# Moving the weight and token tiles of a TensorE-bound encoder step to other byte offsets in SBUF

## The chip, the core and the metric

The kernel runs on one core of one Trainium2 chip. The metric is device time in microseconds of one execution. A core has a matrix engine (PE, with its weight loads shown apart as PEld), three elementwise engines (DVE, ACT, POOL), a DMA-issuing engine (SP) and an on-chip memory (SBUF) of 128 partitions. A tile in SBUF has the same byte address in every partition; this document is about that address modulo 256, which it calls the tile's phase.

## The reference, cut to what matters

One layer of a hybrid encoder is applied to 288 tokens, 256 of a new stream and 32 of a running one. In float32 it computes

```
proj = rmsnorm(x) @ w_in                      2048 -> 5664 columns
pool = trailing means of u, times w_pool      4 groups of 256
ssd  = convolution, chunked scan, gate        32 heads
x    = x + rmsnorm([pool, ssd] @ w_out)       3072 -> 2048
up   = rmsnorm(x) @ w_up                      2048 -> 11264
x    = x + rmsnorm((silu(gate) * val) @ w_down)   5632 -> 2048
```

and the new states. Nearly all arithmetic is in four products of 288 tokens with large weights; every weight is used once.

## The kernel before, in words

**The products.** Tokens lie along the moving side of the matmul, 288 at a time; a 128x128 block of weights is the stationary side. Weights and tokens are each split into a high part, rounded to the matmul's format, and a low part, the remainder. One block costs three matmuls (`mm3`, lines 163 to 165): high weights with high tokens, high weights with low tokens, low weights with high tokens. Each of the three issues its own weight load, so the high weights are loaded twice.

```
pe.matmul(out, wh, a[:, 0, :], start=start, stop=False)   # line 163
pe.matmul(out, wh, a[:, 1, :], start=False, stop=False)   # line 164
pe.matmul(out, wl, a[:, 0, :], start=False, stop=stop)    # line 165
```

`project` runs over groups of 256 output columns, then over the inner dimension in stretches of up to eight blocks. For each stretch `fetch_w` (line 131, SP's DMA queue) brings the raw weights, and `split_w` makes tiles `whi` (ACT, line 146) and `wlo` (DVE, line 147) of 1024 elements a partition, four blocks each. Tags `raw`, `hi` and `lo` have four buffers each in the pool `wpool`. A `whi` buffer is written again when the matmuls that read it are done. One narrow group of 32 columns (the time steps) goes through `split_narrow`, whose stationary operand holds high and low weights side by side, 64 columns (lines 187, 188).

**The token tiles** are `[128, 2, 288]`: the high part at the tile's start, the low part 1152 bytes on, which is 128 modulo 256. They are called `xn`, `mixs` and `hn` (pool `apool`), `fa` (pool `ffn`), `mixp` and `du` (pool `outp`).

**Where tiles lie.** Pools are laid out one behind the other: `const`, `wpool`, a 128-byte pool `shift`, `apool`, `bpool`, and then a region used in turn by `xin` (start), `mixer`, `outp` and `ffn`. Tile sizes are rounded to 32 bytes. In the program as laid out, `const` ends so that `wpool` begins at 34784; every `raw`, `whi` and `wlo` buffer begins at 224 modulo 256. All token tiles begin at 96, so their high part lies at 96 and their low part at 224. `outp` ends at 229344 bytes and `ffn` at 228832, close to the end of what a partition has.

**Order.** Within an engine instructions run in a fixed order, drawn up by the planner when the program is built. Work at the start that concerns the change: `scan_one` (POOL memsets, lines 230 and 232), `sel`, `pick` and `sel64` (DVE, lines 236 to 239) are made in `const` before the first DMA issues of POOL's queue. They are read in the mixer: `scan_one` by the scan at line 439, `pick` at lines 472 and 473, `sel64` by a matmul at line 475. `state_out` (line 690) copies transposed states to tiles `so`, which SP's queue stores; line 970 does so with `fso`. The squares for the norms go through tiles `sq` (line 608), which POOL adds up (line 609). `fr` is a product tile of the last stage (lines 923, 924 and 1036).

Of the kernel before, what the change touches and what calls it, by code (L numbers as in the profile page):

```python
# [8 lines left out]
F32 = mybir.dt.float32  # L9
F32R = mybir.dt.float32r  # L10
AF = mybir.ActivationFunctionType
ALU = mybir.AluOpType
AX = mybir.AxisListType
# [3 lines left out]
P = 128  # L17
# [4 lines left out]
NT = NP_ + NS  # L22
# [3 lines left out]
HEADS = 32  # L26
# [3 lines left out]
NX = D_SSD // P  # L30
NF = D_FF // P
# [12 lines left out]
def body(  # L44
# [38 lines left out]
    act, dve, pool, pe, sp = nc.scalar, nc.vector, nc.gpsimd, nc.tensor, nc.sync  # L83
# [10 lines left out]
    const = ctx.enter_context(tc.tile_pool(name="const", bufs=1))  # L94
    wpool = ctx.enter_context(tc.tile_pool(name="wpool", bufs=4))
# [8 lines left out]
    def aux(shape, name):  # L104
        return aux_ps.tile(shape, F32, tag="aux", name=name)
# [4 lines left out]
    def btile(name):  # L110
        return bpool.tile([P, NT], F32, tag="b", name=name)

    def split_from(a, src, scale=None):
# [4 lines left out]
        else:  # L118
# [4 lines left out]
                ),  # L123
            )

    ahead = [0]

    def fetch_w(view, kb, nk, c0, nc_):
# [5 lines left out]
    def split_w(raw, kb, nk, nc_, after=()):  # L134

        out = []
        step = min(nk, 1024 // nc_)
        for k in range(0, nk, step):
            n = min(step, nk - k)
            hi = wpool.tile([P, n, nc_], F32R, tag="hi", name="whi")  # L140
            lo = wpool.tile([P, n, nc_], F32R, tag="lo", name="wlo")
            with ExitStack() as order:
                order.enter_context(tc.high_priority(offset=ahead[0]))
                for ins in after:
                    order.enter_context(tc.issue_after(ins.ins))
                act.activation(hi, raw[:, k : k + n, :], AF.Copy)  # L146
                dve.tensor_tensor(lo, raw[:, k : k + n, :], hi.bitcast(F32), op=ALU.subtract)  # L147
            out.append([(kb + k + i, hi[:, i, :], lo[:, i, :]) for i in range(n)])
        return out
# [17 lines left out]
    def project(view, groups, acts, ksplit, before=None, done=None, spare=0, hold=()):  # L167
# [9 lines left out]
        for i, (kb, n) in enumerate(ksplit):  # L177
            raws = [fetch_w(view, kb, n, c0, w) for c0, w in groups]
            nxt = None
            if before and i + 1 < len(ksplit):  # L180
                nxt = before(*ksplit[i + 1])
            m0 = 0
            for raw, (c0, w) in zip(raws, groups):
                if w < P:
                    for k, both in split_narrow(raw, kb, n, w, after or ()):
                        o = accs[m0][: 2 * w, :]
                        pe.matmul(o, both, acts[k][:, 0, :], start=k == k_first, stop=False)
                        pe.matmul(o, both, acts[k][:, 1, :], start=False, stop=k == k_last)
                    continue
                parts = split_w(raw, kb, n, w, ((after or ()) if m0 else ()) + (hold if i else ()))  # L190
                for q, part in enumerate(parts):
                    for m in range(w // P):
                        c = slice(m * P, (m + 1) * P)
                        for k, hi, lo in part:
                            mm3(accs[m0 + m], hi[:, c], lo[:, c], acts[k], k == k_first, k == k_last)
                        if done and i + 1 == len(ksplit) and q + 1 == len(parts):
                            done(m0 + m, accs[m0 + m])
                m0 += w // P
            after = nxt
# [13 lines left out]
    ident = const.tile([P, P], F32, name="ident")  # L213
# [12 lines left out]
    rec = const.tile([P, 16], F32, name="rec")  # L226
    for t in range(16):
        pool.memset(rec[:, t : t + 1], 1.0 / (t + 1))
    scan_one = const.tile([HEADS, NT], F32, name="scan_one")
    pool.memset(scan_one, 1.0)  # L230
    for c in range(0, NT, 64):
        pool.memset(scan_one[:, c : c + 1], 0.0)
    sel = const.tile([HEADS, 2], F32, name="sel")
    pick = const.tile([HEADS, NX], F32, name="pick")
    id32 = ident[:HEADS, :HEADS]
    dve.tensor_reduce(sel, id32.rearrange("h (t r) -> h r t", r=2), axis=AX.X, op=ALU.add)
    dve.tensor_reduce(pick, id32.rearrange("h (t r) -> h t r", r=2), axis=AX.X, op=ALU.add)
    sel64 = const.tile([HEADS, 2, 64], F32, name="sel64")
    dve.tensor_copy(sel64, sel.unsqueeze(2).broadcast_to([HEADS, 2, 64]))

    NE = 4
    ebuf = []
    for i in range(NE):
# [120 lines left out]

    mixer = ExitStack()
    mp = mixer.enter_context(tc.tile_pool(name="mixer", bufs=1))
    sc_stage = const.tile([P, 2, 3, NXC], F32, name="sc_stage")
    np_stage = const.tile([P, 2, 15, NU], F32, name="np_stage")
    hist_c = pb[:, 0:60].rearrange("p (r t) -> p r t", t=NXC)
# [43 lines left out]
    def htile(name, n=NT, tag=None):  # L413
        return mp.tile([HEADS, n], F32, tag=tag or name, name=name, bufs={"z": 4}.get(tag, 2) if tag else 1)
# [23 lines left out]
    r = htile("r", tag="z")  # L438
# [42 lines left out]
    for i in range(4):  # L481
        o = btile("bc")
# [201 lines left out]
    def state_out(stage, n, outs, pool_):  # L684

        for s in range(2):
            p_ = aux([n, P], "pso")
            pe.transpose(p_, stage[:, s, :], ident)
            o = pool_.tile([P, P], F32, tag="so", bufs=2, name="so")
            act.activation(o[:n, :], p_, AF.Copy)  # L690
            sp.dma_start(out=outs[s], in_=o[:n, :])

# [46 lines left out]
    def pool_group(i):  # L739
        raw = fetch_w(wpv, 2 * i, 2, 0, 256)  # L740
        wq = split_w(raw, 0, 2, 256)[0]
        for j in range(2):
            o = acc_ps.tile([P, NT], F32, tag="acc", name="acc")
            c = slice(j * P, (j + 1) * P)
            for k, hi, lo in wq:
                mm3(o, hi[:, c], lo[:, c], uin[2 * i + k], k == 0, k == 1)
            a = op_.tile([P, 2, NT], F32R, name=f"mixp{2 * i + j}")
            split_from(a, o, p_scale[:, 2 * i + j : 2 * i + j + 1])
            mix[2 * i + j] = a
# [46 lines left out]
    for gi in range(2):  # L796
        c = slice(gi * P, (gi + 1) * P)
# [46 lines left out]
    for grp in ((0, 1), (2,), (3,), (4,), (5,), (6,), (7,)):  # L844
        project(
            wov, [(256 * c, 256) for c in grp], mix, [(8, 8), (16, 8), (0, 8)],
            mix_before(grp[0]), lambda m, p_: mix_out(p_),
        )
        if grp[0] < 6:
            for t in range(LATE * (grp[0] - 2) // 4, LATE * (grp[0] - 1) // 4) if grp[0] else ():  # L850
                state_mm(t, *state_in(t))
        elif grp[0] == 6:
            late_in = [state_in(t) for t in range(LATE, NX)]
        if grp[0] == 0:
            sp.dma_start(out=xT, in_=xT_d)
            state_out(sc_stage.rearrange("p s r t -> p s (r t)"), 60, (rows4(new_sconv_p), rows4(new_sconv_s)), op_)
            state_out(np_stage.rearrange("p s r t -> p s (r t)"), 120, (rows4(new_pool_p), rows4(new_pool_s)), op_)
# [10 lines left out]
    for s in range(KD + 1):  # L868
# [3 lines left out]
        if s:  # L872
            t = s - 1
            a = atile("hn")
            hi = act.activation(a[:, 0, :], x1[t], AF.Copy, scale=g_ffn_pre[:, t : t + 1])
            lo = dve.scalar_tensor_tensor(  # L876
                a[:, 1, :], x1[t], g_ffn_pre[:, t : t + 1], a[:, 0, :].bitcast(F32),
                op0=ALU.mult, op1=ALU.subtract,
            )
# [16 lines left out]
    fp = ffn.enter_context(tc.tile_pool(name="ffn", bufs=1))  # L896
# [60 lines left out]
    part = []  # L957
    up_half(0, HALF)
    for m in range(0, KD, 2):
        for p_ in project(wdv[:, 0:HALF, :], [(m * P, 256)], f[:HALF], [(0, 8), (8, 8), (16, 6)]):  # L960
            o = btile("part")
# [3 lines left out]
    for s, o_ in enumerate((new_fconv_p, new_fconv_s)):  # L965
        p_ = aux([2 * NF, 2, P], "pfo")
        for r_ in range(2):
            pe.transpose(p_[:, r_, :], fc_stage[:, s, r_, :], ident)
        so = fp.tile([2 * NF, 2, P], F32, tag="fso", bufs=1, name="fso")
        act.activation(so, p_, AF.Copy)  # L970
        sp.dma_start(out=o_.rearrange("o b r (t p) -> t (o b r) p", p=P), in_=so)

# [6 lines left out]
    for q in range(4):  # L979
        for b in range(2):  # L980
            t = apool.tile([P, 512], F32, tag="a", name="xr")
# [126 lines left out]
```

## Time and profile before

| what | value |
|---|---|
| median of 3 runs | 1377.21 us (1376.95 to 1377.78) |
| the profiled execution, its own time | 1377.7 us |
| its span in the profile | 1376.0 us |
| granted PE clock, mean | 0.994 |
| PE busy | 1355.0 us, 98% |
| DVE busy | 879.3 us, 64% |
| ACT busy | 670.8 us, 49% |
| POOL busy | 240.8 us, 18% |

A matmul's duration in the profile overlaps with the next matmul's, so what tells PE's speed is the distance from one matmul's start to the next one's, or the count of matmuls in a window in which PE never idles. Below, this distance is called the step.

### The profile page before, as it was taken

What the parts mean: (1) busy time and instruction counts of PE and PEld (TensorE: products, weight loads), DVE (VectorE), ACT (ScalarE), POOL (GpSimd) and SP (SyncE); (2) the same over time, 40 slices, a digit from 0 to 9 for tenths busy, and PEclk for the clock granted to TensorE, in tenths of its full rate; (3) what the DMA queues carried; (4) which work ended last, traced back from release to release, by engine and by line L of the source; (5) the groups of instructions that cost most, each with busy time, mean ns of one, the idle gap of its engine ahead of it and who ended that gap; (6) DMA issues with size and microseconds to landing.
All of it is one profiled execution on the core that took longest, in us unless ns stands there. A gap on an engine that the chain in (4) does not pass through costs nothing.

```text
span 1376.0 us, 25874 instructions
## 1 busy us (share of the span) xinstructions
PE 1355.0 (98%) x10247; PEld 1333.0 (97%) x10247; DVE 879.3 (64%) x1551; ACT 670.8 (49%) x1013; POOL 240.8 (18%) x394
## 2 busy tenths in 40 slices
PE   8999999999999999999999999999999999999996
PEld 7999999999999998999999999999999999999995
DVE  6898887669544448877667653334766766654443
ACT  6547767546444345644444443334444444454441
POOL 3122211122123310212112100000211211201110
PEclk9999999999999999999999999999999999999998
DMA  8878875455755634766555455555555545476662
GB/s 270 258 194 262 250 207 171 152 187 176 228 179 175 191 106 146 223 176 194 175 157 178 149 169 169 169 170 161 176 161 171 167 156 181 155 230 184 191 186 86
DMA packets 293287, 250.55 MB, mean 182 GB/s; under 512 B 67344, under 2 KB 286458, under 8 KB 293038
## 3 DMA queue, kind: packets, MB, share of 16 engines
q1 hardware_dynamic: 289962, 242.41, 57.8%
q0 software_dynamic: 2320, 3.86, 0.9%
q10 hardware_dynamic: 884, 2.63, 0.5%
q8 instruction: 80, 1.31, 0.4%
q14 instruction: 41, 0.34, 0.1%
HBM read 234.55 MB, written 14.31 MB: 181 GB/s over the span
## 4 chain that ended last, share of the span: by engine, by line
PE 97%; DVE 2%; issue 0%; DMA 0%; ACT 0%; DVEq 0%
PE acc L163 31%; PE acc L165 31%; PE acc L164 30%; PE pst L824 1%; PE py L555 1%; DVE wlo L147 0%; DVE xr L1066 0%; DVE hn L876 0%; PE py L559 0%; PE py L561 0%; PE py L557 0%; DVE xsum L888 0%; DMA xt<-in_x_prompt 0%; PE pt L299 0%; PE pt L301 0%
## 5 line engine op out<-in xcount | busy, mean ns | idle before, releaser
L147 DVE TENSOR_TENSOR wlo<-raw,whi 128x1024 fp32r<-128x1024 f32 (+1 forms) x414 | 493.9, 1194 | 351.2 <-ACT whi L146 349.8
L146 ACT ACTIVATE whi<-raw 128x1024 fp32r<-128x1024 f32 (+1 forms) x414 | 427.1, 1033 | 518.6 <-PE acc L164 424.8
L163 PE MATMUL acc<-hn,whi 128*128 128x288 f32 x1392 | 409.0, 297 | 2.3 <-ACT whi L146 2.3
L165 PE MATMUL acc<-hn,wlo 128*128 128x288 f32 x1392 | 410.0, 296 | 0.9 <-DVE wlo L147 0.9
L164 PE MATMUL acc<-hn,whi 128*128 128x288 f32 x1392 | 405.4, 292 | 0.0
L163 PEld LDWEIGHTS acc<-hn,whi 128*128 128x128 f32 x1392 | 260.9, 188 | 3.5 <-ACT whi L146 3.4
L165 PEld LDWEIGHTS acc<-hn,wlo 128*128 128x128 f32 x1392 | 260.9, 188 | 1.9 <-DVE wlo L147 1.8
L164 PEld LDWEIGHTS acc<-hn,whi 128*128 128x128 f32 x1392 | 262.2, 188 | 0.2 <-DVE hn L876 0.2
L163 PE MATMUL acc<-xn,whi 128*128 128x288 f32 x704 | 210.1, 300 | 0.0
L163 PE MATMUL acc<-fa,whi 128*128 128x288 f32 x704 | 208.5, 296 | 0.0
L165 PE MATMUL acc<-fa,wlo 128*128 128x288 f32 x704 | 207.4, 295 | 0.0
L165 PE MATMUL acc<-xn,wlo 128*128 128x288 f32 x704 | 207.0, 296 | 0.0
L164 PE MATMUL acc<-xn,whi 128*128 128x288 f32 x704 | 206.8, 295 | 0.0
L164 PE MATMUL acc<-fa,whi 128*128 128x288 f32 x704 | 205.3, 292 | 0.0
L163 PEld LDWEIGHTS acc<-xn,whi 128*128 128x128 f32 x704 | 132.6, 189 | 0.7
L164 PEld LDWEIGHTS acc<-xn,whi 128*128 128x128 f32 x704 | 132.8, 189 | 0.3
L164 PEld LDWEIGHTS acc<-fa,whi 128*128 128x128 f32 x704 | 132.3, 188 | 0.0
L163 PEld LDWEIGHTS acc<-fa,whi 128*128 128x128 f32 x704 | 132.3, 188 | 0.0
L165 PEld LDWEIGHTS acc<-xn,wlo 128*128 128x128 f32 x704 | 131.9, 188 | 0.3
L165 PEld LDWEIGHTS acc<-fa,wlo 128*128 128x128 f32 x704 | 131.7, 187 | 0.0
L909 POOL COPY fc_stage<-ebuf 128x4 f32<-128x4 f32 x88 | 27.5, 312 | 506.0 <-DVE ebuf L908 506.0
L905 POOL COPY ebuf<-pf 128x2 f32<-128x2 f32 x88 | 74.5, 847 | 117.9 <-DVE fc L915 54.0
(308 smaller groups left out, 1635.0 us busy)
## 6 DMA issues: line engine op xcount, KB each, us to landing
raw<-in_w_up SPq DMA_DIRECT2D x82, 1024.0 KB, 5.1
raw<-in_w_in SPq DMA_DIRECT2D x40, 1024.0 KB, 5.6
raw<-in_w_down SPq DMA_DIRECT2D x32, 1024.0 KB, 5.4
raw<-in_w_out SPq DMA_DIRECT2D x24, 1024.0 KB, 5.4
raw<-in_w_down SPq DMA_DIRECT2D x16, 768.0 KB, 4.6
gb<-g_d SPq DMA_DIRECT2D x8, 832.0 KB, 4.9
raw<-in_w_up SPq DMA_DIRECT2D x12, 512.0 KB, 3.6
raw<-in_w_in SPq DMA_DIRECT2D x6, 512.0 KB, 6.4
```

Of the source, the lines that this page charges most:

```text
L146: act.activation(hi, raw[:, k : k + n, :], AF.Copy)
L147: dve.tensor_tensor(lo, raw[:, k : k + n, :], hi.bitcast(F32), op=ALU.subtract)
L163: pe.matmul(out, wh, a[:, 0, :], start=start, stop=False)
L164: pe.matmul(out, wh, a[:, 1, :], start=False, stop=False)
L165: pe.matmul(out, wl, a[:, 0, :], start=False, stop=stop)
L555: pe.matmul(y[c, 0:256], xw[:, 0, c], m[:, j, 0:256], start=True, stop=False)
L824: ins = pe.matmul(st[:, o, :], x_, w, start=i != 1, stop=i != 0)
L905: pool.tensor_copy(e[:, 258:260], pf[:, 4:6, i])
L909: pool.tensor_copy(fc_stage[:, :, :, i], e[:, 256:324].rearrange("p (s c) -> p s c", c=34)[:, :, 0:2])
```

## The change

The change moves data in SBUF and leaves the arithmetic as it is.

- High and low weight tiles come from a helper `wtile`. Each buffer is 1088 elements instead of 1024 (256 bytes more), and the data begin 2 elements (8 bytes) into it for high parts, 34 elements (136 bytes) for low parts.
- `scan_one`, `sel`, `pick` and `sel64` leave `const` for the pool `mixer`, and are made after the start-up pool is closed. `const` is shorter by 1152 + 32 + 64 + 512 = 1760 bytes, so `wpool` begins at 33024, which is 0 modulo 256. High weights then lie at 8, low weights at 136. `wpool` is longer by 8 buffers of 256 bytes, so everything behind it moves by 2048 - 1760 = 288 bytes: token tiles begin at 128, their low part at 0.
- To make room, `so` uses the buffers of tag `sq`, and `fso` those of tag `fr`.

```diff
+    def wtile(part, n, nc_):
+
+        t = wpool.tile([P, 1024 + 64], F32R, tag=part, name="w" + part)
+        d = 2 if part == "hi" else 34
+        return t[:, d : d + n * nc_].rearrange("p (k c) -> p k c", k=n)
+
...
-            hi = wpool.tile([P, n, nc_], F32R, tag="hi", name="whi")
-            lo = wpool.tile([P, n, nc_], F32R, tag="lo", name="wlo")
+            hi = wtile("hi", n, nc_)
+            lo = wtile("lo", n, nc_)
...
-    scan_one = const.tile([HEADS, NT], F32, name="scan_one")
...
-    sel = const.tile([HEADS, 2], F32, name="sel")
-    pick = const.tile([HEADS, NX], F32, name="pick")
...
-    sel64 = const.tile([HEADS, 2, 64], F32, name="sel64")
-    dve.tensor_copy(sel64, sel.unsqueeze(2).broadcast_to([HEADS, 2, 64]))
...
     mp = mixer.enter_context(tc.tile_pool(name="mixer", bufs=1))
+    scan_one = mp.tile([HEADS, NT], F32, name="scan_one")
+    pool.memset(scan_one, 1.0)
+    for c in range(0, NT, 64):
+        pool.memset(scan_one[:, c : c + 1], 0.0)
+    sel = mp.tile([HEADS, 2], F32, name="sel")
+    pick = mp.tile([HEADS, NX], F32, name="pick")
...
+    sel64 = mp.tile([HEADS, 2, 64], F32, name="sel64")
+    dve.tensor_copy(sel64, sel.unsqueeze(2).broadcast_to([HEADS, 2, 64]))
...
-            o = pool_.tile([P, P], F32, tag="so", bufs=2, name="so")
+            o = pool_.tile([P, NT], F32, tag="sq", bufs=2, name="so")[:, :P]
...
-        so = fp.tile([2 * NF, 2, P], F32, tag="fso", bufs=1, name="fso")
+        so = fp.tile([P, NT], F32, tag="fr", bufs=2, name="fso")[: 2 * NF, : 2 * P].rearrange("p (r c) -> p r c", r=2)
```

More of the change, by code (lines that the diff above doesn't have):

```diff
@@ L228, in body @@
         pool.memset(rec[:, t : t + 1], 1.0 / (t + 1))
-    scan_one = const.tile([HEADS, NT], F32, name="scan_one")
-    pool.memset(scan_one, 1.0)
-    for c in range(0, NT, 64):
-        pool.memset(scan_one[:, c : c + 1], 0.0)
-    sel = const.tile([HEADS, 2], F32, name="sel")
-    pick = const.tile([HEADS, NX], F32, name="pick")
-    id32 = ident[:HEADS, :HEADS]
-    dve.tensor_reduce(sel, id32.rearrange("h (t r) -> h r t", r=2), axis=AX.X, op=ALU.add)
-    dve.tensor_reduce(pick, id32.rearrange("h (t r) -> h t r", r=2), axis=AX.X, op=ALU.add)
-    sel64 = const.tile([HEADS, 2, 64], F32, name="sel64")
-    dve.tensor_copy(sel64, sel.unsqueeze(2).broadcast_to([HEADS, 2, 64]))
     NE = 4
@@ L366, in body @@
     mp = mixer.enter_context(tc.tile_pool(name="mixer", bufs=1))
+    scan_one = mp.tile([HEADS, NT], F32, name="scan_one")
[4 more added lines that the diff above has]
+    pick = mp.tile([HEADS, NX], F32, name="pick")
+    id32 = ident[:HEADS, :HEADS]
+    dve.tensor_reduce(sel, id32.rearrange("h (t r) -> h r t", r=2), axis=AX.X, op=ALU.add)
+    dve.tensor_reduce(pick, id32.rearrange("h (t r) -> h t r", r=2), axis=AX.X, op=ALU.add)
+    sel64 = mp.tile([HEADS, 2, 64], F32, name="sel64")
+    dve.tensor_copy(sel64, sel.unsqueeze(2).broadcast_to([HEADS, 2, 64]))
     sc_stage = const.tile([P, 2, 3, NXC], F32, name="sc_stage")
```

## The prediction

> **What bounds the kernel now.** First the engines' totals and the list of who waited for whom:
>
> ```profile
> PE 1355.0 (98%) x10247; PEld 1333.0 (97%) x10247; DVE 879.3 (64%) x1551; ACT 670.8 (49%) x1013; POOL 240.8 (18%) x394
> ```
>
> ```profile
> PE pt L281 <- POOL ebuf L245: 3.6, 1, 3.6
> PE acc L163 <- ACT whi L146: 2.3, 5, 0.7
> PE pt L299 <- DVE xT L304: 1.4, 1, 1.4
> PE acc L165 <- DVE wlo L147: 0.9, 3, 0.5
> PE psum_f L1019 <- ACT fsq L1036: 0.2, 1, 0.2
> ```
>
> PE has work for 98% of the span, and all its waits for others come to 8.4 us. The groups of PE instructions say what the work is; the three lines of `mm3` for one kind of token tile:
>
> ```profile
> L165 PE MATMUL acc<-hn,wlo 128*128 128x288 f32 x1392 | 410.0, 296 | 0.9 <-DVE wlo L147 0.9
> L163 PE MATMUL acc<-hn,whi 128*128 128x288 f32 x1392 | 409.0, 297 | 2.3 <-ACT whi L146 2.3
> L164 PE MATMUL acc<-hn,whi 128*128 128x288 f32 x1392 | 405.4, 292 | 0.0
> ```
>
> With the 704 of `xn`, 704 of `fa`, 256 of `mixs`, 128 of `mixp`, 16 of `du` and 16 that accumulate in `acc_x`, each line has 3,216 matmuls: 9,648 in all. Durations overlap, so the step comes from windows in which PE never idles:
>
> ```profile
> core 0: us, PE busy (x) PEld busy (x) DVE busy (x) ACT busy (x) POOL busy (x), PEclk, DMA share, GB/s
> 0.00:20.00 20.00, 14.93 (x87) 12.94 (x87) 12.41 (x26) 8.78 (x17) 11.96 (x52) 1.00 0.90 279
> 20.00:42.00 22.00, 22.00 (x159) 20.38 (x158) 13.93 (x30) 16.24 (x26) 1.48 (x4) 1.00 0.83 255
> 42.00:112.00 70.00, 70.00 (x526) 68.92 (x526) 64.03 (x146) 39.94 (x67) 15.92 (x24) 1.00 0.80 239
> ...
> 780.00:900.00 120.00, 120.00 (x910) 120.00 (x909) 54.91 (x67) 46.62 (x59) 5.49 (x9) 1.00 0.55 168
> 900.00:1130.00 230.00, 230.00 (x1741) 230.00 (x1741) 139.90 (x229) 103.67 (x136) 32.89 (x56) 1.00 0.52 167
> ```
>
> 230 us / 1741 = 132.1 ns; 120 / 910 = 131.9 ns. DVE is 46% busy in the one and 61% in the other, and the step stays: it isn't set by what other engines do to memory. 9,648 x 132.1 ns = 1274 us of the 1376.0 us span. So the change is worth what it does to this step, and 1 ns of step is 9.6 us, 0.7% of the time. About 0.2%, or 2.8 us, is what a measurement of this kernel can tell from no change; that is 0.3 ns of step.
>
> Now the timeline of PE alone, start and duration in us, in the steady part:
>
> ```profile
> 820.76 0.30 PE L163 MATMUL acc<-fa,whi 128*128 128x288 f32 x1
> 820.90 0.29 PE L164 MATMUL acc<-fa,whi 128*128 128x288 f32 x1
> 821.02 0.29 PE L165 MATMUL acc<-fa,wlo 128*128 128x288 f32 x1
> 821.15 0.29 PE L163 MATMUL acc<-fa,whi 128*128 128x288 f32 x1
> 821.29 0.29 PE L164 MATMUL acc<-fa,whi 128*128 128x288 f32 x1
> 821.42 0.30 PE L165 MATMUL acc<-fa,wlo 128*128 128x288 f32 x1
> 821.55 0.30 PE L163 MATMUL acc<-fa,whi 128*128 128x288 f32 x1
> ...
> 1359.43 0.30 PE L164 MATMUL acc<-fa,whi 128*128 128x288 f32 x1
> 1359.56 0.29 PE L165 MATMUL acc<-fa,wlo 128*128 128x288 f32 x1
> ```
>
> The steps are 0.14, 0.12, 0.13, then 0.14, 0.13, 0.13. The same form of matmul takes 0.12 in one place and 0.14 in another, with nothing to wait for, so part of the 132 ns is stall inside PE. Over the whole trace, leaving out steps over 145 ns, the means are 135.1 ns from L163 to L164 (3,116 steps), 129.4 ns from L164 to L165 (3,156 steps; the last pair of rows above is the last of them), 131.9 ns from L165 to L163 (3,094 steps). The single steps cluster near 126, 132 and 138 ns.
>
> **The change part by part.** *The phases.* While one matmul streams its tokens, the weights of the next are loaded. In the kernel before, the three steps pair tokens and weights at (96, 224), (224, 224), (96, 224): half of 256 apart, together, half apart. Afterwards they are (128, 8), (0, 136), (128, 8): the weights lie 136 beyond the tokens in all three. No row has weights off a multiple of 32, or this distance. What the rows can bound: from 126 ns, the shortest cluster of steps, to 137 ns, the lower edge of the longest. Against the present 132.2 (the mean of the three kinds) that is -6.2 to +5 ns. One more row shows how little the length of the weight load matters: the narrow group loads 64 columns instead of 128,
>
> ```profile
> 37.42 0.30 PE L187 MATMUL acc<-xn,both 128*64 128x288 f32 x1
> 37.55 0.29 PE L188 MATMUL acc<-xn,both 128*64 128x288 f32 x1
> 37.69 0.29 PE L187 MATMUL acc<-xn,both 128*64 128x288 f32 x1
> 37.81 0.29 PE L188 MATMUL acc<-xn,both 128*64 128x288 f32 x1
> 37.95 0.29 PE L187 MATMUL acc<-xn,both 128*64 128x288 f32 x1
> ```
>
> and four steps take 0.53 us, 132 ns each. So a stall that grows with the bytes of the weight load isn't seen; one that depends on where the streams begin relative to each other, or on where the token stream begins in memory, is left. I take 129.4 ns, the mean of the fastest of the three kinds of step, for all of them: a uniform distance should make the three alike, and the trace shows a whole kind of step running at that speed. Gain 132.2 - 129.4 = 2.8 ns.
>
> [...]
>
> How many matmuls gain: until 42 us PE has 87 + 159 records in windows with the DMA engines 83 to 90% busy, so I give that stretch nothing. 9,648 - 246 = 9,400 matmuls x 2.8 ns = 26 us. Others must keep up: from 42 to 112 us DVE works 64.03 us of 70, and a step shorter by 2.1% makes the window 68.5, by 4.7% 66.7; both are still above 64.
>
> *Writers of the shifted tiles.* ACT and DVE now write at 8 and 136, and DVE reads the former. The convolutions read at offsets of 4 and 8 bytes:
>
> ```profile
> L915 DVE SCALAR_TENSOR_TENSOR fc<-ebuf,pf,fc 128x290 f32<-128x290 f32 x176 | 90.5, 516 | 3.5 <-ACT fc L913 0.7
> L121 DVE SCALAR_TENSOR_TENSOR xn<-pt,g,xn 128x288 fp32r<-128x288 f32 x16 | 8.2, 513 | 7.4 <-ACT xn L120 7.4
> ```
>
> 516 ns for 290 elements against 513 for 288 aligned ones: nothing. Were a write 10% dearer, some 24 `wlo` of 1.2 us in that tight window would add 3 us to DVE's 64, still under 68. Zero. The weights' DMAs land at 0 instead of 224 and have slack after 42 us; zero.
>
> *The constants made later.* POOL and DVE at the start:
>
> ```profile
> 1.61 0.17 DVE L236 TENSOR_REDUCE sel<-ident 32x2 f32<-32x32 f32 x1 [1.61 <-POOL ident masks.py:199]
> 1.72 0.17 DVE L237 TENSOR_REDUCE pick<-ident 32x16 f32<-32x32 f32 x1
> 1.82 2.12 DVE L239 COPY sel<-sel 32x128 f32<-32x128 f32 x1
> 2.30 0.33 POOL L230 MEMSET scan_one<- 32x288 f32 x1
> 0.81 3.08 DMA xt<-in_x_prompt
> ```
>
> Taking 0.33 us off POOL's queue ahead of its parameter DMAs, and 2.5 us off DVE, gains nothing on the path: the chain of waits begins with the DMA of `xt`, landed at 3.89 us. Made behind start-up, about 42 us, the same DVE work goes into the window with 6 us of DVE slack; POOL has 54 us there. Behind it on DVE stand the `wlo` splits that PE needs. `pick` is first read at 53.6 us and `scan_one` at 95.1. Cost zero; with the cover gone, 2.5 us.
>
> *`so` in the buffers of `sq`, `fso` in those of `fr`.*
>
> ```profile
> 379.40 0.39 ACT L608 ACTIVATE sq<-acc 128x288 f32<-128x288 f32 x1
> 379.69 0.50 ACT L791 ACTIVATE mg<-acc,pb 128x288 f32<-128x288 f32 x1
> 380.07 0.45 ACT L690 ACTIVATE so<-pso 120x128 f32<-120x128 f32 x2
> 381.83 1.06 ACT L146 ACTIVATE whi<-raw 128x1024 fp32r<-128x1024 f32 x1 [1.31 <-PE acc L164]
> ```
>
> New waits: the copy to `so` waits for POOL's addition of the square before it (1.5 us each), and the next square waits for `so` to be stored (at most 5.3 us to landing). Behind it on ACT stands the next `whi`, and PE behind that. Cover: ACT runs ahead until PE frees a buffer, three tiles of 24 matmuls, 3 x 24 x 132 ns = 9.5 us, against 5.3 + 3 us at worst. Zero; with the cover gone, about 5 us. `fso` waits 2.0 us once today and has two buffers then; zero.
>
> **Sum.** 1377.7 us of the profiled execution - 26 = 1351.4; the runs' median lies 0.5 us lower: 1351.
>
> **The rivals.**
>
> *No change.* The steps are set by something that phases don't touch. For it: in the trace (96, 224) occurs twice, at 135.1 and at 131.9 ns, so the same phases don't have one price, and the first two steps together make 264.5 = 2 x 132.2, as if a constant rate were only unevenly divided. 1377, with 2.8 us to either side. [...]
>
> *Slower: the step in which tokens and weights lie together is the fast one.* Taken literally, the trace has 129.4 ns for (224, 224) and 133.5 as the mean of the two steps half of 256 apart. The change puts the middle step about half apart too. Price 133.5 - 132.1 = 1.4 ns on all, 9,400 x 1.4 = 13 us: 1390. It decides once the new distance is over 0.3 ns dearer than today's mean. Weights off the 32-byte grid could be dearer still: all steps in the longest cluster's neighbourhood, +5 ns, give 1424. Against it: the unequal (96, 224) steps.
>
> *Faster by more.* All steps at 126 ns: 9,400 x 6.2 = 58 us, 1319. For it, only that single steps reach this.
>
> **How the numbers follow.** Faster 0.52: 0.40 near my 1351 (1330 to 1374), 0.12 near 1319. No change 0.10, since a step that varies between clusters will hardly land within 0.3 ns when every phase moves. Slower 0.38: 0.26 near 1390, 0.12 beyond 1396. The range leaves out the last and about half of the far faster case: 1318 to 1396. The likeliest case's own range is 1330 to 1374.
>
> **What would show it.** Right: the window 780 to 900 us, or its counterpart, holds about 927 matmuls instead of 910; the three kinds of step come closer together; counts and durations of `whi` and `wlo` stay. Wrong: 910 as before (phases don't matter), or 900 and fewer (the new distance costs), or new rows of PE waiting for `whi` or `wlo` (ACT held up behind `so`, DVE behind the constants). What would make it wrong is above all the untested 8 bytes.

## The result, and the profile after

The changed kernel takes 1369.0 us (median; 1368.7 to 1369.3) against 1377.1 us before: a ratio of 0.9941, 95% interval 0.9924 to 0.9958. That is 8 us faster, 0.6%, where 26 us were forecast: the right way, a third of the size.

The windows of the changed kernel (columns as in the prediction; the three are those quoted there):

```profile
42.00:112.00 70.00, 70.00 (x533) 69.23 (x532) 66.05 (x150) 37.98 (x56) 18.04 (x30) 1.00 0.76 234
...
780.00:900.00 120.00, 120.00 (x917) 120.00 (x916) 53.49 (x64) 47.65 (x60) 4.67 (x8) 1.00 0.52 162
900.00:1130.00 230.00, 230.00 (x1757) 230.00 (x1756) 143.37 (x237) 104.90 (x140) 34.54 (x60) 1.00 0.52 171
```

917 matmuls where there were 910, and 1757 for 1741: the step is 0.8 to 0.9% shorter in these two stages. 927 would have been the forecast. Earlier the gain is smaller: 0.6% from 270 to 510 us (132.11 to 131.30 ns) and 0.2% from 112 to 270 us (131.69 to 131.42). Over all steps under 145 ns between matmuls of `mm3` the records give 131.23 ns (9,492 steps) against 132.14 (9,488). 9,500 x 0.91 ns = 8.6 us; the two spans differ by 8.8 us (1376.0 and 1367.2). So the step explains the gain, and next to nothing is left for other causes. PE's list of waits is what it was:

```profile
PE pt L275 <- POOL ebuf L239: 3.6, 1, 3.6
PE acc L169 <- ACT whi L152: 2.2, 4, 0.7
PE pt L293 <- DVE xT L298: 1.4, 1, 1.4
PE acc L171 <- DVE wlo L153: 0.9, 3, 0.5
PE psum_f L1024 <- ACT fsq L1041: 0.2, 1, 0.2
```

And the timeline of PE alone after the change (start and duration in us; lines 169 to 171 are the former 163 to 165):

```profile
820.30 0.29 PE L169 MATMUL acc<-fa,whi 128*128 128x288 f32 x1
820.42 0.29 PE L170 MATMUL acc<-fa,whi 128*128 128x288 f32 x1
820.56 0.30 PE L171 MATMUL acc<-fa,wlo 128*128 128x288 f32 x1
820.69 0.29 PE L169 MATMUL acc<-fa,whi 128*128 128x288 f32 x1
820.82 0.29 PE L170 MATMUL acc<-fa,whi 128*128 128x288 f32 x1
820.95 0.30 PE L171 MATMUL acc<-fa,wlo 128*128 128x288 f32 x1
```

Three steps take 0.39 us (820.30 to 820.69, and 820.56 to 820.95), where they took 0.39 and 0.40 in turn. To the nanosecond the three kinds now take 127.1, 131.8 and 134.8 ns in the mean, and over nine in ten of each kind lie within 1.2 ns of that. They have not become alike, though all three have the same distance: (128, 8), written as (tokens, weights) in bytes modulo 256, appears as 127.1 and as 134.8.

### The profile page after: what moved, and what is told of

The parts are those of the page before. It is cut to its first block, busy times and chain, and to the rows that moved or that the text cites. A ratio compares the mean times of both kernels' runs of the same rounds, so it can differ in the third digit from the quotient of the medians.

```text
span 1367.2 us, 25869 instructions
## 1 busy us (share of the span) xinstructions
PE 1346.3 (98%) x10247; PEld 1323.7 (97%) x10247; DVE 878.0 (64%) x1551; ACT 671.0 (49%) x1013; POOL 249.5 (18%) x394
## 4 chain that ended last, share of the span: by engine, by line
PE 97%; DVE 2%; issue 0%; DMA 0%; ACT 0%; DVEq 0%
PE acc L171 31%; PE acc L170 31%; PE acc L169 30%; PE pst L829 1%; PE py L560 1%; DVE wlo L153 0%; DVE xr L1071 0%; DVE hn L881 0%; PE py L564 0%; PE py L566 0%; PE py L562 0%; DVE xsum L893 0%; DMA xt<-in_x_prompt 0%; PE pt L293 0%; PE pt L295 0%
## 5 line engine op out<-in xcount | busy, mean ns | idle before, releaser
L153 DVE TENSOR_TENSOR wlo<-raw,whi 128x1024 fp32r<-128x1024 f32 (+1 forms) x414 | 494.0, 1194 | 346.2 <-ACT whi L152 344.9
L152 ACT ACTIVATE whi<-raw 128x1024 fp32r<-128x1024 f32 (+1 forms) x414 | 427.7, 1034 | 516.7 <-PE acc L170 422.5
L169 PEld LDWEIGHTS acc<-xn,whi 128*128 128x128 f32 x704 | 133.3, 190 | 0.5
L171 PEld LDWEIGHTS acc<-xn,wlo 128*128 128x128 f32 x704 | 132.6, 189 | 0.5
L170 PEld LDWEIGHTS acc<-xn,whi 128*128 128x128 f32 x704 | 132.5, 188 | 0.4
L171 PEld LDWEIGHTS acc<-fa,wlo 128*128 128x128 f32 x704 | 132.2, 188 | 0.0
L170 PEld LDWEIGHTS acc<-fa,whi 128*128 128x128 f32 x704 | 131.7, 187 | 0.0
```

## The experiments

The theory under test: the step is set by where the token stream and the loading weights lie in SBUF. The two do run at the same time: in the trace before, the load of L164's weights begins at 820.76 us, as L163's matmul does, and takes 0.19 us of its 0.30. Rivals: the gain comes from the other edits; from the tokens' own place; from the 8 bytes by themselves. In what follows a pair (tokens, weights) gives phases modulo 256 for the three steps in turn, and "d" is the offset in elements that `wtile` uses. "Half a turn" is 128 bytes, half of 256. Below each run stands, where a reading rests on it, its count of matmuls in the 200 us from 900 to 1100 us; before, there are 1514 (132.1 ns a step), after the change 1528 (130.9).

### Is it the phases at all (e1, e2)?

e1 keeps the later constants and the shared buffers, and fills `const` up so that all phases are the old ones:

```diff
-        t = wpool.tile([P, 1024 + 64], F32R, tag=part, name="w" + part)
-        d = 2 if part == "hi" else 34
+        t = wpool.tile([P, 1024], F32R, tag=part, name="w" + part)
+        d = 0
...
+    hole = const.tile([P, 440], F32, name="hole")
+    pool.memset(hole[:, 0:1], 0.0)
```

> The changed kernel with weights and tokens back at their old phases: tokens 96 and 224, all weights 224; only the later constants and the shared buffers of so and fso are left of the change. If the gain of 8 us comes from phases, this takes the 1377 us of before and its step is 132.1 to 132.2 ns. If it comes from the shorter start, it takes 1369 us with the step of before.

Measured: 1378.5 us against 1378.0 us before, ratio 1.0001 (0.9990 to 1.0011), step 132.12 ns.

```profile
900.00:1100.00 200.00, 200.00 (x1515) 200.00 (x1514) 120.10 (x196) 90.48 (x119) 28.14 (x48) 1.00 0.52 168
```

The other edits are worth nothing.

e2 is the changed kernel with `d = 0` for both parts, so that everything lies 32 bytes on from before and the distances are the old ones.

> The changed kernel with all weights at 0 and tokens at 128 and 0: against before, everything lies 32 bytes further on and the distances of weights and tokens are those of before (128, 0, 128). If the distance decides (the theory of the prediction), 1377 us and a step of 132.2 ns. If the tokens' own phase (on the 128-byte grid) decides, 1369 us and 131.2 ns.

Measured: ratio 0.9996 (0.9984 to 1.0008), step 132.15 ns, and the same three kinds of step as before: 135.1, 129.4, 132.0 (before 135.1, 129.4, 131.9).

```profile
900.00:1100.00 200.00, 200.00 (x1515) 200.00 (x1514) 120.74 (x196) 89.22 (x117) 28.14 (x48) 1.00 0.52 168
```

Moving both streams together by 32 bytes changed nothing here (132.15 ns against 132.14); putting the tokens on a multiple of 128 bytes is not the gain.

### What of the distance counts (e3, e4, e8)?

```diff
-        d = 2 if part == "hi" else 34
+        d = 0 if part == "hi" else 32     # e3: (128, 0), (0, 128), (128, 0)
+        d = 46 if part == "hi" else 14    # e4: (128, 184), (0, 56), (128, 184)
+        d = 2                             # e8: (128, 8), (0, 8), (128, 8)
```

> The changed kernel without the 8 bytes: high weights at 0, low at 128, tokens at 128 and 0, distance 128 in all three steps. If it takes a uniform distance of half of 256 and the 8 bytes add nothing, 1369 us; if the 8 bytes are what matters, 1377 us; if being half apart is the slow case, as the slower rival had it, 1385 us or more.

Measured: 1391.3 us, ratio 1.0086 (1.0065 to 1.0108), step 133.29 ns. The windows of e3:

```profile
780.00:900.00 120.00, 120.00 (x902) 120.00 (x901) 57.87 (x76) 48.48 (x63) 7.59 (x12) 1.00 0.52 163
900.00:1100.00 200.00, 200.00 (x1502) 200.00 (x1501) 115.31 (x182) 87.55 (x115) 25.41 (x44) 1.00 0.51 166
```

902 matmuls in 120 us. With a distance of 128 in all three steps the kernel is slower than before, and 8 bytes more make it faster than before: 22 us lie between e3 and the change.

> The changed kernel with weights 56 beyond the tokens in all three steps (high at 184, low at 56, tokens at 128 and 0). The first sweep has 136.7 ns there against 131.1 at 136. If phases alone set the step of the whole kernel, this is 5.5 ns x 9,648 = 53 us slower than the changed kernel: 1422 us. If the kernel's step depends on more than phases (the other engines' traffic), it falls well short of that.

Measured: 1390.1 us, ratio 1.0093 (1.0062 to 1.0124), step 133.28 ns.

```profile
900.00:1100.00 200.00, 200.00 (x1502) 200.00 (x1501) 115.66 (x184) 87.61 (x114) 25.42 (x44) 1.00 0.51 167
```

Slower than before, but by 12 us and not 45: the forecast from the series missed. The number came from a series in which both token parts had the same phase; in e4 they are 128 apart, and later series with the kernel's own layout give 133.2 and 133.4 ns (m3, m5). So the other engines' traffic isn't needed to explain the shortfall. Here a step held for a layout, not for a distance alone: at distance 56 it was 136.6 ns in that series and 133.28 in e4.

> The changed kernel with low weights at 8 as well, so that the pairs of tokens and loading weights are (128, 8), (0, 8), (128, 8). If it is the 8 bytes on the two half-apart steps that bring the gain, 1369 to 1372 us; if all three steps must have the same distance, 1377 us or more.

Measured: ratio 1.0006 (0.9996 to 1.0015), step 132.31 ns.

```profile
900.00:1100.00 200.00, 200.00 (x1515) 200.00 (x1514) 120.74 (x196) 89.25 (x117) 28.14 (x48) 1.00 0.51 168
```

Taken with e2, e3 and the change itself this is a square of four: offsets 0/0 give 132.15 ns, 8/8 give 132.31, 0/128 give 133.29, 8/136 give 131.23. These four kernels differ in `d` alone. The 8 bytes alone change the step by 0.2 ns, the half turn of the low weights alone costs 1.1 ns, both together gain 0.9. Neither part of the change has a price of its own.

### TensorE alone (m1 to m5)

These kernels run only matmuls, in `mm3`'s order on fixed tiles, one source line for each series, so that a series costs microseconds and a whole map fits into one run:

```python
wh = hi[:, h // 4 + 256 * q + 128 * m :][:, :128]
x0 = tok[:, a0 // 4 + STRIDE * k :][:, :288]
for o, w, x, s, e in seq(128, 0, 8, 136): keep(pe.matmul(o, w, x, start=s, stop=e))
```

> TensorE alone: series of 96 matmuls in the order of the kernel (high-high, high-low, low-high, 16 blocks, 2 column halves) on fixed tiles, each series with other phases; everything else of the computation is left out and the outputs are filled with zeros. The first and last series have the phases of before and after. If phases alone make the step, they repeat 132.2 and 131.2 ns here. With both token parts at 0 and both weights at x, x going from 0 to 248 by 8, the theory of distance expects a step that changes with x by a nanosecond or more and is low at 136; if the distance doesn't matter, all are within 0.3 ns. Series at distance 136 and 0 with tokens at 8, 16, 32, 64, 96 and 128: equal to those with tokens at 0 if only the distance counts, else the absolute phase counts.

Measured: the first and last series repeat the kernels: 132.1 and 132.3 ns at the phases of before, 131.2 and 131.2 at those of after (the token tiles lie 2816 bytes apart here, 2304 in the kernels; m4 and m5 take that up). With tokens at 0, the step over x runs from 131.1 or 131.2 (x = 48, 80, 88, 136, 144) through 133.3 (most) to 136.6 (x = 56), in jumps and not in a smooth curve. Moving tokens and weights together by 32, 64, 96 or 128 changes nothing (131.6 to 131.7 at distance 0, 131.2 at 136); by 8 or 16 it does (133.2 and 130.7 at distance 0).

> TensorE alone again, 258 series of 48 matmuls, the rest of the computation left out and the outputs zeros: both token parts at t, all weights d further on, t = 0, 4, 8, 12, 16, 20, 24, 28 and d = 0 to 248 by 8. If only the distance counts, the eight values of t give the same curve over d. If the place within 32 bytes counts too, as the first sweep hints (131.7 at 0, 133.3 at 8, 130.7 at 16, all at distance 0), the curves differ, and t = 16 holds the lowest steps, 130 ns or less. If the step is bound by something else near 131 ns, nothing lies below 130.

Measured, 32 distances in each row:

| tokens at t within 32 | mean step, ns | lowest | highest |
|---|---|---|---|
| 0 | 132.8 | 131.1 | 136.3 |
| 4 | 135.9 | 133.3 | 144.4 |
| 8 | 133.9 | 130.2 | 138.3 |
| 12 | 132.1 | 130.0 | 136.7 |
| 16 | 132.2 | 130.0 | 134.6 |
| 20 | 135.4 | 132.1 | 140.1 |
| 24 | 134.0 | 130.0 | 136.7 |
| 28 | 130.5 | 129.3 | 133.3 |

The place of the tokens counts too, and not a little: the means differ by 5.4 ns, the distances within a row by 4 to 11. The lowest steps are at 28, not at 16 as expected. Means go 4, 8, 0, 12 from dear to cheap within each half of 32, which suggests a period of 16 bytes (0 and 16 differ by 0.6 ns, 4 and 20 by 0.5, 8 and 24 by 0.1), though 28 is 1.6 ns cheaper than 12. Why these places differ no run here shows.

> TensorE alone, 258 series of 48 matmuls, the rest of the computation left out and the outputs zeros; token tiles exactly as in the kernel (low part 1152 bytes on, tiles 2304 bytes apart). Tokens begin at 128 or at 156 (28 within 32 bytes); high weights at x = 0 to 252 by 4, low weights at x + 128 or at x. The theory after the grid is that a step is a beat between two read streams, set by the place of the tokens within 32 bytes first (28: about 130 ns) and by the distance second. It expects the mean over x to be near 130 ns for 156 and 2 to 3 ns higher for 128, and x = 8 with low at 136 among the best few for 128. A theory in which the distance decides alone expects the two token places to have the same curve, shifted by 28.

Measured: tokens at 156, mean 131.3 and 131.5 ns, and 91 of 128 series under 131.2; tokens at 128, mean 132.5 and 132.8, and 12 of 128. So the order of the two places is as expected, the difference half of it. With low weights half a turn on, x = 8 is the lowest of all 64 offsets for tokens at 128 (131.1 ns), with two more within 0.1 ns of it; with low weights at the same x as high ones, x = 240 gives 130.15. So the change sits on the best place of its own arrangement, though not of its token place.

> TensorE alone, 133 series of 96 matmuls, the rest of the computation left out and the outputs zeros. (1) The exact addresses of before and after, two series each: 132.2 and 131.2 ns if phases set the kernel's step. [...] (3) 32 or 64 weight columns: if the stall is a collision with the weight load, the step falls by several ns; if it belongs to the token stream, it stays within 1 ns. (4) Output at other offsets of its bank: no change expected. (5) Token tiles 2560 bytes apart with the low part 1280 bytes on, tokens at 156, 140 and 128, all weights at x: 130 ns for many x at 156 if the place within 32 bytes counts most.

Measured, with high-part matmuls of four series as the profile groups them; all four have tokens at 0 and weights at 136 (the fourth and fifth number are the first and last start; 94 steps lie between):

```profile
L64 PE MATMUL acc<-tok,hi x64: 272/274/300, 102.4 to 112.9; 128*128 128x192 f32 x64
L66 PE MATMUL acc<-tok,hi x64: 277/282/284, 123.8 to 134.9; 128*128 128x256 f32 x64
L72 PE MATMUL acc<-tok,hi x64: 292/296/298, 196.2 to 208.5; 128*128 128x288 f32 x64
L79 PE MATMUL acc<-tok,hi x64: 288/294/295, 289.1 to 301.4; 128*32 128x288 f32 x64
```

10.5, 11.1 and 12.3 us for 192, 256 and 288 columns: 111.7, 118 and 131 ns. To the nanosecond, 128, 192 and 224 columns all take 111 to 112, 256 take 118.0, 272 take 125.0, 304 take 138.7. Between 256 and 304 columns that is 0.43 ns a column, though in uneven stages: 312 and 320 columns take 146.5 and 146.7. What sets the floor up to 224 columns no run tested, and how much of the 131 ns at 288 is a cost of each matmul these series don't tell. Phases moved the step by 3.9 ns between the slowest and the fastest whole kernel (133.29 in e3, 129.36 in e9). 32 columns of weights instead of 128 (line 79) leave the step of 288 columns at 131.1, 64 at 131.6: it isn't the bytes of the weight load. Other offsets of the output give 131.1 each. With the low part 1280 bytes on, tokens at 156 take 130.5 ns in the mean of 32 offsets, 19 of them 130.0 or less; tokens at 140 take 132.1 and at 128 132.8, as expected.

(1) missed: at the exact phases of before the series run at 131.2, not 132.2, while those of after agree. Hence the last set.

> TensorE alone, 30 series of 192 matmuls (15, each twice), the rest of the computation left out and the outputs zeros. The phases of seven whole kernels, this time modulo 512 as in their programs (tokens of before at 96 + 512n, all its weights at 480; in the changed kernel and its variants the weights' buffers alternate between both halves of 512), and of before and of weights at 0 with other halves of 512. If addresses alone make the step, the series give 132.1 for before, 131.2 for after, 132.15 with weights at 0, 133.3 at distance 128, 133.3 at 56, 132.3 with low weights at 8, 130.0 for e7. If before and weights at 0 still come out at 131.0 to 131.2 as in the series until now, the kernel's step holds something that the series lacks.

Measured, series against whole kernel, in ns:

| phases of | series | kernel |
|---|---|---|
| before | 131.1 | 132.1 |
| after | 131.2 | 131.2 |
| e2, weights at 0 | 132.2 | 132.15 |
| e3, distance 128 | 133.3 | 133.3 |
| e4, distance 56 | 133.4 | 133.3 |
| e8, low weights at 8 | 132.6 | 132.3 |
| e7, below | 130.0 | 130.0 |
| e9, below | 129.3 | 129.4 |

Three of the series (high-part matmuls, 190 steps from first to last start; 0.1 us of rounding is 0.5 ns a step), for before, e3 and e9:

```profile
L59 PE MATMUL acc<-tok,hi x128: 291/295/298, 66.7 to 91.7; 128*128 128x288 f32 x128
L65 PE MATMUL acc<-tok,hi x128: 288/295/300, 218.0 to 243.4; 128*128 128x288 f32 x128
L69 PE MATMUL acc<-tok,hi x128: 290/290/292, 319.6 to 344.2; 128*128 128x288 f32 x128
```

Seven of eight agree within 0.3 ns, though the other engines are idle in the series (ACT and POOL work in the first of 40 slices alone, and behind it DMA moves 1 to 4 GB/s): addresses on PE alone are enough to make these steps. Before doesn't agree, whichever half of 512 the weights lie in (131.1 four times). Its phases are those of e2 moved by 32, and in the series that move matters here (131.1 against 132.2), while the kernels before and e2 are equal. Nor do phases modulo 256 fix a step by themselves: tokens at 128 and all weights at 0, low part 1152 bytes on, took 131.2 ns in m3 and 132.2 here, where the tokens lie 256 bytes further on in their buffer and there are 16 token tiles instead of 8. What else of the addresses or of the history decides there stays open.

### Can it be had cheaper (e5, e6, e7, e9)?

e5 puts the tokens 28 bytes into their tiles and drops `wtile`:

```diff
+    def ttile(pool_, **kw):
+        t = pool_.tile([P, 2 * NT + 8], F32R, **kw)
+        return t[:, 7 : 7 + 2 * NT].rearrange("p (r c) -> p r c", r=2)
...
-            hi = wtile("hi", n, nc_)
+            hi = wpool.tile([P, n, nc_], F32R, tag="hi", name="whi")
```

> The changed kernel without the offsets of its weight tiles (high and low at 0), and with tokens 28 bytes into their tiles; token tiles are then 2336 bytes and begin at every multiple of 32, so the distance takes many values. If the place within 32 bytes counts most, the step falls from 131.2 to about 130.4 ns, the mean of the grid's column t = 28, and this takes 7 to 8 us less than the changed kernel: 1361 us. If the distance alone counts, the mean over distances is about 132.8 ns, the grid's column t = 0, and it takes 1384 us.

Measured: 1375.4 us, ratio 0.9987 (0.9977 to 0.9997), step 131.87 ns. Better than the distance alone would have it (1384 us), worse than the place alone (1361): the grid's mean for this place, 130.5 ns, doesn't carry over. The low part lies 128 from the high one here, which the grid lacks and m3 has (131.3 and 131.5 ns in the mean at this place); and with tiles of 2336 bytes the distance changes from token tile to token tile, which no series has.

e7 therefore gives all token parts one phase and all weights another. It needs tiles of 2560 bytes and makes room by three raw buffers and the mask `tri` in the mixer; e6 is the control for the buffers.

```diff
-    shift_t = shift.tile([P, 32], F32, name="shift_t")
+    shift_t = shift.tile([P, 24], F32, name="shift_t")
+    def ttile(pool_, **kw):
+        return pool_.tile([P, 2, 320], F32R, **kw)[:, :, 7 : 7 + NT]
...
-        d = 2 if part == "hi" else 34
+        d = 21 if part == "hi" else 21    # e7: weights at 84, tokens at 124
+        d = 63 if part == "hi" else 63    # e9: weights at 252, tokens at 124
...
-        raw = wpool.tile([P, nk, nc_], F32, tag="raw", name="raw")
+        raw = wpool.tile([P, nk, nc_], F32, tag="raw", bufs=3, name="raw")
```

> The changed kernel with three buffers for raw weights instead of four, and nothing else: a control for the next. Expected 1369 us if two loads in flight are enough; more if the start, where the DMA engines are 80 to 90% busy, needs the fourth.

Measured: 1368.2 us, ratio to before 0.9930 (0.9914 to 0.9947), step 131.22 ns: the control is the changed kernel.

> The changed kernel with every token part at 124 (28 within 32 bytes; tiles of 2560 bytes, low part 1280 bytes on) and all weights at 84, the same distance of 216 in every step; three raw buffers and the triangle mask in the mixer make the room. The grid has 129.98 ns at that place: 1.2 ns under the changed kernel's step, so 11 to 12 us less than its control, 1358 us. If a kernel's step can't be read from the series, it comes out at 131 ns or more, 1369 us.

Measured: 1357.3 us, ratio 0.9855 (0.9840 to 0.9869), step 130.00 ns; the three kinds of step take 130.0 each, in the mean.

```profile
900.00:1100.00 200.00, 200.00 (x1540) 200.00 (x1540) 124.16 (x206) 91.86 (x121) 29.62 (x52) 1.00 0.52 168
```

> As e7, with the weights at 252 instead of 84: distance 128 in place of 216. The grid and the fourth set of series have 129.33 ns there, the lowest of all places. If the series carry over, 0.67 ns x 9,500 = 6 us less than e7: 1351 us. If 130.0 is the least that a kernel reaches, 1357 us.

Measured: 1350.2 us, ratio 0.9799 (0.9782 to 0.9815), step 129.36 ns, 19 us less than the change under study. The windows of e9:

```profile
780.00:900.00 120.00, 120.00 (x930) 120.00 (x929) 51.11 (x57) 46.74 (x58) 2.86 (x5) 1.00 0.54 171
900.00:1100.00 200.00, 200.00 (x1548) 200.00 (x1548) 127.35 (x212) 92.84 (x123) 30.98 (x55) 1.00 0.52 171
```

1548 matmuls in 200 us against 1502 in e3: 129.2 and 133.2 ns. The steps of e7 and e9 were read off the series before these kernels ran; that of e3 was not.

## Why the prediction was wrong, point by point

**The bound** held. PE's step was what counted, other engines' traffic doesn't set it (in m5 seven of eight kernels' steps come out within 0.3 ns with the other engines idle), and 9.6 us a nanosecond is what the runs show: from e3 to e9 the step falls by 3.93 ns and the span of the profiled execution by 38.0 us (1388.3 to 1350.3), 9.7 us a nanosecond.

**The size of the step's gain failed.** The prediction took "129.4 ns, the mean of the fastest of the three kinds of step, for all of them", since "a uniform distance should make the three alike". The term, -2.8 ns and -26 us, measured -0.91 ns and -8.6 us. Two things were wrong in it. One kind of step has no price by its phases: (128, 8) takes 127.1 ns in one place of the triple and 134.8 in another, and only the mean over the triple can be read as a cost. The trace of before said so already, with (96, 224) at 135.1 and at 131.9; the prediction used this against its rivals and not against its own term. Nor does "a whole kind of step" run at 129.4 ns there: of the 3,156 steps from L164 to L165, 1,409 take 125 or 126 ns and 1,488 take 132 or 133, and the term is the mean of the two. And a uniform distance isn't enough: 128 throughout costs 1.15 ns (e3), -40 throughout gains 2.1 (e7), 128 throughout with other tokens gains 2.8 (e9). So the direction came right by luck, as far as the reason given for it goes: of the kernels with the change's token place and one distance throughout, e3 (128) and e4 (56) are slower than before, and only the change's 136 is faster.

**The slower rival** (half of 256 apart is dear) was right about the distance that it named: e3 took 133.29 ns and 1391 us, where the rival said 133.5 ns and 1390. It fell to the 8 bytes, which the prediction named as untested. How it came by 133.5, as a mean of two kinds of step, was no better founded than the 129.4.

**The no-change rival** read the uneven steps as a division of one rate, and the trace after the change fits that: behind 553 us a triple takes 393 or 394 ns nearly every time, while its steps differ by 8 ns. It was wrong that phases don't touch the rate: e3 and the change, which differ in `d` alone, are 1.6% apart in the step, e3 and e9 3.0%.

**Writers of the shifted tiles: zero**, held. ACT's 414 splits took 1034 ns in the mean (1033 before), DVE's 1194 (1194 before).

**The later constants: zero**, held (e1). `sel`, `pick` and `sel64` are made at 52 to 54 us, and `pick` is read at 54.6 (53.6 before). The copy of `sel` takes 0.21 us there; at the start it had taken 2.12.

**`so` in the buffers of `sq`: zero**, held. The changed kernel, for the tile `so`:

```profile
L695 ACT ACTIVATE so<-pso x4: 261/266/278, 379.8 to 386.0; 60x128 f32<-60x128 f32 x2, 120x128 f32<-120x128 f32 x2
  POOL msum L614: 1.1, 1
  DMA out<-so: 0.2, 1
```

ACT waited 1.1 us for POOL's addition and 0.2 us for the store of an earlier `so`. The prediction had waits of this kind, but longer, and PE's list of waits shows none of them.

**DVE from 42 to 112 us** had room for the gain: 66.05 of 70 us, which is 2 us more than before. e9 shows the room at its end, with 0.8 us of PE waiting for DVE's `tok` in front of the matmul with `sel64`.

## What to carry to other kernels

Where a trace shows PE busy for 98% with steps of uneven length, the addresses of its two streams are worth a trial: here they moved the step by 3% between the worst and the best kernel. The effect didn't add up: the 8 bytes alone changed the step by 0.2 ns, the half turn of the low weights alone cost 1.1, and together they gained 0.9. Don't price kinds of step within a repeating group one by one; price the group. A run of bare matmul series maps hundreds of places at once, and with the kernel's own layout, stride and order it repeats seven of eight whole kernels within 0.3 ns. Used as a forecast, before the kernel ran, it hit e7 and e9 and missed e4 and e5, whose layouts it didn't have; so confirm in the kernel.

## What the runs showed that was not expected

The step comes in few values: 129.3, 130.0, 131.1, 131.7, 132.2, 133.3 and 136.7 ns return in series after series, at places that have nothing visible in common; nearly two thirds of the series of 288 columns lie within 0.1 ns of one of them. The whole kernels keep to such values as well. From 553 to 1340 us three steps together take 400.0 ns in e3 and in e4, whose distances differ, 396.7 before and in e1 and e2, 393.4 after and in e6, and 390.0 in e7: each 3.3 or 3.4 ns from the next. e5, e8 and e9 (395.5, 396.8 and 388.0) don't keep to that spacing. Why the step keeps to such values no run here shows. Tokens 28 bytes past a multiple of 32 ran faster than aligned ones at each of the 32 distances (130.5 against 132.8 ns in the mean). And from 128 to 224 columns the step didn't change with the columns: 128, 192 and 224 all took 111 to 112 ns (m4).
